# Differential values of an encoder trunk: one token tile after the other, high and low weight halves side by side

## The chip, the cores and the metric

The kernel runs on one core of a Trainium2 chip. The metric is the device time in microseconds (us). Before the change it is 1755.69 us, the median of 3 runs (1755.67 to 1756.33).

The core has a matrix engine (TensorE, PE), which multiplies a stationary 128x128 operand with a moving operand of up to 512 columns and adds the result up in PSUM; a vector engine (VectorE, DVE); a scalar engine (ScalarE, ACT); GpSimd (POOL); and SyncE (SP), which here issues most of the DMAs. PEld in the profile is the loading of the stationary operand, which lies beside PE's products.

## The reference

The program is a trunk of two layers over 512 tokens and a model width of 1024. In each layer differential attention, a convolution module and a neighbourhood attention run on the same normalised input, are merged by gates, and an FFN follows. The change touches one part, the values of the differential attention (4 heads of 128 columns):

```python
h = rmsnorm(x, norm)                       # 512 x 1024
va = (h @ w_in)[:, 1024:1536]              # values, 512 x 512: 4 heads x 128
v = va.reshape(B, S, HA, DV_A).transpose(0, 2, 1, 3)
...
a = softmax(q1 k1) - lam * softmax(q2 k2)  # for each head
o = einsum('bhqk,bhkd->bhqd', a, v)
```

The kernel computes a float32 product from fp32r operands: each operand is split into a high and a low half (`split`), and three products are added up, high by high, high by low and low by high.

## The kernel before

**Tiles.** The normalised input `self.h` is held as 8 chunks of 128 model columns (KD = 8), each as a high and a low half of 128 x 512 tokens, all in SBUF. `values` (L605 and below) computes the values of two heads, 256 columns, for all 512 tokens; `diff_v` calls it for group 0 (heads 0 and 1) and group 1 (heads 2 and 3). With two layers that is 4 calls. In each call the tokens are four tiles of 128; a tile's high or low half of one chunk is the stationary operand, and 256 columns of weights stream past it.

**The weights of a call** are 8 chunks of 128x256. `weights` loads four of them with one DMA (512 KB) into a raw buffer `wr`, and `split` makes the high half `wh` with a copy on ACT (L143) and the low half `wl` with a subtraction on DVE (L157). There are three buffers of each of `wr`, `wh` and `wl`, used in turn by all parts of the layer; a buffer is free once its last reader is done. A call takes two of each.

**The loops of a call.** The accumulators are two PSUM buffers `mm` of 128 x 2 x 256, each for two token tiles; there are three `mm` buffers in all. With the first four chunks the loop runs over the two accumulators, the chunks and the tiles of the accumulator; with the last four over chunks and then all four tiles. For each chunk and tile there are three products of 256 columns: L621 high tokens by `wh`, L623 high tokens by `wl`, L625 low tokens by `wh`. After the last one, four copies on ACT and four subtractions on DVE move the sums from PSUM into `v`, as a high and a low half of 256 columns each.

**What sets the order.** PE's order is the one that the program is written in (its schedule is manual). The order of ACT, DVE, POOL and SP comes from a scheduler by priorities; the load and split of weights have a priority that is up to 400 places ahead of where they are written (`high_priority`). The attention is cut into pieces that run from a queue: `chunk` counts, and every fourth `chunk` calls `tick`, which lets a waiting piece of attention issue its instructions between the products. `values` calls `chunk` 16 times, so there are 4 ticks in a call.

**What stands around a call.** In each layer the order is the projections of differential head 0 (`diff_in`: Q, then K), the values of group 0, head 1, a gate (`gate_c`), head 2, the values of group 1, head 3. In the first call the pieces are those of the neighbourhood attention (`natten_unit`): scores (L800), which DVE adds to a bias and reduces (L719), exponentials and scalings on ACT (`natten_b`, `natten_e`), transposes on PE, their copies `natten_pt` as a high half on ACT and a low half on DVE, and the product with its values on PE (L745, `natten_av`, `natten_mm`). In the second call they are those of the differential attention (`diff_sc`, `diff_av`). DVE also runs the taps of the convolution (`conv_z`, L160) and the rotation of Q and K (`diff_rp`, `diff_t`).

Of the kernel before, what the change touches and what calls it, by code (L numbers as in the profile page):

```python
# [11 lines left out]
F32 = mybir.dt.float32  # L12
F32R = mybir.dt.float32r
I32 = mybir.dt.int32
AF = mybir.ActivationFunctionType
ALU = mybir.AluOpType
# [4 lines left out]
P = 128  # L21
# [5 lines left out]
KD = 8  # L27
# [34 lines left out]
class Net:  # L62
# [539 lines left out]

        yield from self.norm(st[0], CB, (3, 1), done)

    def values(self, ap, parts):  # L605


        mm = self.nc.tensor.matmul
        accs = [self.ps("mm", (P, 2, 256)) for _ in range(2)]
        for o in range(0, KD, 4):  # L610
            wh, wl = self.weights(ap[:, o * 256:(o + 4) * 256], 1024)
            both = [(k, t) for k in range(o, o + 4) for t in range(4)]
            if o == 0:

                both.sort(key=lambda kt: kt[1] // 2)
            for n, (k, t) in enumerate(both):
                s = slice((k - o) * 256, (k - o + 1) * 256)
                out = accs[t // 2][:, t % 2, :]
                ts = slice(t * P, (t + 1) * P)

                mm(out, self.h[k][:, 0, ts], wh[:, s], start=k == 0 and t % 2 == 0,  # L621
                   stop=False, skip_group_check=True)
                mm(out, self.h[k][:, 0, ts], wl[:, s], start=False, stop=False,  # L623
                   skip_group_check=True)
                mm(out, self.h[k][:, 1, ts], wh[:, s], start=False,  # L625
                   stop=k == KD - 1 and t % 2 == 1, skip_group_check=True)
                if n % 2:
                    self.chunk()
        vs = []
        for acc in accs:  # L630
            v = self.sb("v", [P, 2, 512], F32R)
            for t in range(2):
                for hi, lo, a in parts(v[:, t], acc[:, t]):
                    self.split(hi, lo, a)
            vs.append(v)
        return vs

    def natten_in(self, pr, st, ys):
# [190 lines left out]

    def diff_v(self, g, st):  # L830
        self.phase = "diff"
        st["v", g] = self.values(self.a["w_va"][self.i, g], lambda v, a: ((v[:, 0:256], v[:, 256:512], a),))

    def diff_unit(self, head, qt, st4, k2, st, box, ys):

# [686 lines left out]
```

## Time and profile before

| | |
|---|---|
| median of 3 runs | 1755.69 us |
| profiled execution | 1756.09 us |
| its span in the profile | 1754.3 us |
| DMA, mean over the span | 145 GB/s |
| products on PE | 8970 |

The profiled execution is 1.8 us longer than its span, which counts from the first to the last instruction. The granted clock of PE is in the highest tenth in all 40 slices of the span. In rows of the timeline the first number is the start, the second the duration, both in us; "f32 x8" at the end means that eight instructions of one form stand in one row, and the brackets give the idle time before the row and what ended it. A product is drawn from its start to its modelled end, so that products overlap; the distance from one start to the next is the time that it takes in the stream.

In the rows of the windows each window has its length, then for PE, PEld, DVE, ACT and POOL the busy time in us with the number of instructions, then the granted clock, the share of DMA and its GB/s.

### The profile page before, as it was taken

Reading aid. Unit: us, or ns where it says so; the run is one execution under the profiler, and the core shown is the slowest. Engines: PE = TensorE matmul, PEld = TensorE weight load, DVE = VectorE, ACT = ScalarE, POOL = GpSimd, SP = SyncE. Lnnn points to the kernel's source line nnn. Section 1 sums busy time; section 2 is a strip of 40 time slices with the busy share of each in tenths; the row PEclk is TensorE's granted clock in tenths of the full one; section 3 lists DMA queues with packets and bytes.
Section 4 is the critical chain, followed back from the end, with each engine's and each line's share of the span. In section 5 each row is a group of like instructions: output and inputs, shape, how many; then the busy total and the mean of one; then the engine's idle time right before and its main releaser. Section 6 shows DMA issues by size and latency. Waiting matters only on the chain.

```text
span 1754.3 us, 25072 instructions
## 1 busy us (share of the span) xinstructions
PE 1747.3 (100%) x8970; PEld 1490.2 (85%) x8970; DVE 1421.7 (81%) x2346; ACT 964.4 (55%) x1729; POOL 104.0 (6%) x114
## 2 busy tenths in 40 slices
PE   9999999999999999999999999999999999999998
PEld 7888888888888888888888898888888988888887
DVE  7967987998799687797776688889887985977876
ACT  5566545226577275574545665553365763745654
POOL 0000000000121020100000000000001210101000
PEclk9999999999999999999999999999999999999999
DMA  6575641334767365543446655323256764755332
GB/s 230 159 192 158 162 126 46 112 100 140 230 162 186 118 171 155 142 119 131 156 130 164 194 150 153 111 73 96 93 176 199 183 172 121 179 143 157 96 105 97
DMA packets 114781, 253.82 MB, mean 145 GB/s; under 512 B 16864, under 2 KB 23776, under 8 KB 114656
## 3 DMA queue, kind: packets, MB, share of 16 engines
q1 hardware_dynamic: 101264, 227.83, 42.3%
q0 software_dynamic: 12672, 23.07, 8.1%
q8 instruction: 71, 1.16, 0.3%
q10 hardware_dynamic: 720, 1.31, 0.2%
q14 instruction: 54, 0.44, 0.1%
HBM read 215.46 MB, written 7.34 MB: 127 GB/s over the span
## 4 chain that ended last, share of the span: by engine, by line
PE 97%; DVE 1%; DMA 1%; ACT 1%; SPq 0%; issue 0%; POOL 0%; POOLq 0%; ACTq 0%; DVEq 0%
PE ffn_mm L1013 6%; PE ffn_sc L1013 6%; PE ffn_mm L180 4%; PE ffn_mm L179 4%; PE ffn_mm L181 4%; PE ffn_mm L1016 3%; PE ffn_sc L1016 3%; PE mergea_mm L180 2%; PE mergea_mm L181 2%; PE mergea_mm L179 2%; PE ffn_tr L1013 2%; PE natten_mm L179 2%; PE natten_mm L180 2%; PE gateb_mm L180 2%; PE gateb_mm L181 2%; PE gateb_mm L179 2%
## 5 line engine op out<-in xcount | busy, mean ns | idle before, releaser
L160 DVE SCALAR_TENSOR_TENSOR conv_z<-glu_z,pre_par,conv_z 128x512 f32<-128x512 f32 x240 | 179.6, 748 | 3.4
L143 ACT ACTIVATE ffn_wh<-ffn_wr 128x1024 fp32r<-128x1024 f32 (+1 forms) x92 | 92.7, 1021 | 99.5 <-PE ffn_mm L180 63.4
L157 DVE TENSOR_TENSOR ffn_wl<-ffn_wr,ffn_wh 128x1024 fp32r<-128x1024 f32 (+1 forms) x92 | 107.1, 1175 | 20.8 <-ACT ffn_wh L143 20.4
L979 POOL DMA_DIRECT2D ffn_qk<-w_fu x88 | 78.0, 992 | 589.3 <-DMA ffn_qk<-w_fu 323.7
L143 ACT ACTIVATE mergea_wh<-mergea_wr 128x1024 fp32r<-128x1024 f32 (+1 forms) x32 | 27.1, 846 | 96.8 <-PE mergea_mm L180 79.6
L157 DVE TENSOR_TENSOR ffn_t<-ffn_mm,wo_rb 128x512 f32<-128x512 f32 (+1 forms) x46 | 31.1, 677 | 51.6 <-PE ffn_mm L181 51.6
L157 DVE TENSOR_TENSOR ffn_wl<-ffn_qk,ffn_wh 128x1024 fp32r<-128x1024 f32 x44 | 53.7, 1220 | 11.0 <-ACT ffn_wh L143 10.9
L143 ACT ACTIVATE diff_a<-diff_sc,diff_s 128x512 f32<-128x512 f32 x32 | 22.0, 688 | 71.6 <-DVE diff_s L893 71.6
L143 ACT ACTIVATE ffn_wh<-ffn_qk 128x1024 fp32r<-128x1024 f32 x44 | 46.7, 1061 | 26.8 <-PE ffn_mm L180 16.2
L179 PE MATMUL ffn_mm<-ffn_v,ffn_wh 128*128 128x512 f32 x132 | 51.4, 389 | 0.0
L180 PE MATMUL ffn_mm<-ffn_v,ffn_wh 128*128 128x512 f32 x132 | 51.4, 389 | 0.0
L181 PE MATMUL ffn_mm<-ffn_v,ffn_wl 128*128 128x512 f32 x132 | 51.3, 389 | 0.0
L179 PE MATMUL ffn_mm<-ffn_y,ffn_wh 128*128 128x512 f32 x132 | 51.3, 389 | 0.0
L180 PE MATMUL ffn_mm<-ffn_y,ffn_wh 128*128 128x512 f32 x132 | 51.3, 389 | 0.0
L181 PE MATMUL ffn_mm<-ffn_y,ffn_wl 128*128 128x512 f32 x132 | 51.3, 389 | 0.0
L143 ACT ACTIVATE natten_wh<-natten_wr 128x1024 fp32r<-128x1024 f32 x24 | 25.4, 1058 | 42.2 <-issue 15.5
L1013 PE MATMUL ffn_sc<-wo_h,ffn_wh 128*128 128x512 f32 x176 | 48.0, 394 | 0.0
L157 DVE TENSOR_TENSOR ffn_t<-ffn_t,ffn_e 128x256 f32<-128x256 f32 x84 | 46.3, 551 | 1.0 <-ACT ffn_e L143 0.9
L893 DVE TENSOR_REDUCE diff_s<-diff_sc 128x1 f32<-128x512 f32 x64 | 42.1, 683 | 2.2 <-PE diff_sc L800 2.2
L1013 PE MATMUL ffn_mm<-wo_h,ffn_wh 128*128 128x512 f32 x160 | 43.6, 394 | 0.0
L225 POOL TENSOR_TENSOR diff_rc<-diff_sm,pre_power 128x4 f32<-128x4 f32 x8 | 8.9, 1115 | 561.8 <-DVE diff_sm L160 503.2
L143 ACT ACTIVATE natten_b<-natten_b,natten_s 128x256 f32<-128x256 f32 x64 | 30.4, 499 | 20.4 <-DVE natten_s L719 20.3
(894 smaller groups left out, 6050.1 us busy)
## 6 DMA issues: line engine op xcount, KB each, us to landing
ffn_qk<-w_fu POOLq DMA_DIRECT2D x88, 256.0 KB, 6.6
ffn_wr<-w_fg SPq DMA_DIRECT2D x44, 512.0 KB, 4.4
ffn_wr<-w_fd SPq DMA_DIRECT2D x32, 448.0 KB, 3.8
ffn_r<-w_fu SPq DMA_DIRECT2D x44, 256.0 KB, 3.1
ffn_qk<-w_fg SPq DMA_DIRECT2D x44, 256.0 KB, 3.3
ffn_qk<-w_fu SPq DMA_DIRECT2D x44, 256.0 KB, 3.4
natten_wr<-w_in SPq DMA_DIRECT2D x16, 512.0 KB, 4.2
diff_wr<-w_in SPq DMA_DIRECT2D x16, 512.0 KB, 4.3
```

The source lines that it names most:

```text
L143: i = self.nc.scalar.activation(out, in_, func, **kw)
L157: return self.nc.vector.tensor_tensor(out, a, b, op)
L160: return self.nc.vector.scalar_tensor_tensor(out, a, s, b, op0, op1)
L179: mm(out, wh, ah, start=first, stop=False, **kw)
L180: mm(out, wh, al, start=False, stop=False, **kw)
L181: mm(out, wl, ah, start=False, stop=last, **kw)
L225: nc.gpsimd.tensor_tensor(col, ms, self.power, ALU.pow)
L893: nc.vector.tensor_reduce(out=m[:, u:u + 1], in_=sc, op=ALU.max, axis=AX.X, negate=True)
L979: nc.gpsimd.dma_start(q, wu[:, lo], accum_op=ALU.add)
L1013: mm(out, wh[:, c], bs[k][b], start=first and k == 0, stop=False, skip_group_check=True)
L1016: mm(out[:, 0], wl[:, c], bs[k][b][:, 0], start=False, stop=k == 3, skip_group_check=True)
```

## The change

`values` is written anew. The token tile is now the outermost loop. The high and the low half of a weight chunk lie side by side in one buffer of 128 x 2 x 2 x 256 (two chunks a buffer; the buffers tagged `wh` and `wl` hold the first and the second pair of chunks of a load). For each tile the high tokens of the 8 chunks are multiplied with 512 columns (L624), the high and the low weights at once, into a PSUM buffer of 2 x 256; then the low tokens of the 8 chunks with the 256 columns of the high weights (L628), into the first half of it. The two halves are added when the tile is moved out: a copy on ACT (high half of the first 256), a subtraction on DVE, and a further addition on DVE of the second 256 columns. Each tile has its own `mm` buffer, so the third tile takes the buffer of the first. Loads and splits of all weights are written ahead of the loop; a load is split in two pieces of 128 x 2 x 256. There are still 16 calls of `chunk`.

```diff
@@ -602,37 +602,39 @@
 
         yield from self.norm(st[0], CB, (3, 1), done)
 
-    def values(self, ap, parts):
+    def values(self, ap):
 
 
         mm = self.nc.tensor.matmul
-        accs = [self.ps("mm", (P, 2, 256)) for _ in range(2)]
-        for o in range(0, KD, 4):
-            wh, wl = self.weights(ap[:, o * 256:(o + 4) * 256], 1024)
-            both = [(k, t) for k in range(o, o + 4) for t in range(4)]
-            if o == 0:
-
-                both.sort(key=lambda kt: kt[1] // 2)
-            for n, (k, t) in enumerate(both):
-                s = slice((k - o) * 256, (k - o + 1) * 256)
-                out = accs[t // 2][:, t % 2, :]
-                ts = slice(t * P, (t + 1) * P)
-
-                mm(out, self.h[k][:, 0, ts], wh[:, s], start=k == 0 and t % 2 == 0,
-                   stop=False, skip_group_check=True)
-                mm(out, self.h[k][:, 0, ts], wl[:, s], start=False, stop=False,
+        ws = []
+        with self.tc.high_priority(offset=min(self.w_ahead, self.tc.cur_priority - self.p0)):
+            for o in range(0, KD, 4):
+                raw = self.sb("wr", [P, 2, 2, 256])
+                self.nc.sync.dma_start(raw.rearrange("p a b c -> p (a b c)"),
+                                       ap[:, o * 256:(o + 4) * 256])
+                for n, tag in enumerate(("wh", "wl")):
+                    w = self.sb(tag, [P, 2, 2, 256], F32R)
+                    self.split(w[:, :, 0], w[:, :, 1], raw[:, n])
+                    ws += [w[:, k] for k in range(2)]
+        vs = []
+        for t in range(4):
+            out = self.ps("mm", (P, 2, 256))
+            hs = [(a[:, 0, t * P:(t + 1) * P], a[:, 1, t * P:(t + 1) * P]) for a in self.h]
+            for k, (hi, lo) in enumerate(hs):
+                mm(out, hi, ws[k], start=k == 0, stop=False, skip_group_check=True)
+                if k % 4 == 3:
+                    self.chunk()
+            for k, (hi, lo) in enumerate(hs):
+                mm(out[:, 0], lo, ws[k][:, 0], start=False, stop=k == KD - 1,
                    skip_group_check=True)
-                mm(out, self.h[k][:, 1, ts], wh[:, s], start=False,
-                   stop=k == KD - 1 and t % 2 == 1, skip_group_check=True)
-                if n % 2:
+                if k % 4 == 3:
                     self.chunk()
-        vs = []
-        for acc in accs:
-            v = self.sb("v", [P, 2, 512], F32R)
-            for t in range(2):
-                for hi, lo, a in parts(v[:, t], acc[:, t]):
-                    self.split(hi, lo, a)
-            vs.append(v)
+            if t % 2 == 0:
+                v = self.sb("v", [P, 2, 512], F32R)
+                vs.append(v)
+            hi, lo = v[:, t % 2, 0:256], v[:, t % 2, 256:512]
+            self.split(hi, lo, out[:, 0])
+            self.tt(lo, lo.bitcast(F32), out[:, 1], ALU.add)
         return vs
 
     def natten_in(self, pr, st, ys):
@@ -829,7 +831,7 @@
 
     def diff_v(self, g, st):
         self.phase = "diff"
-        st["v", g] = self.values(self.a["w_va"][self.i, g], lambda v, a: ((v[:, 0:256], v[:, 256:512], a),))
+        st["v", g] = self.values(self.a["w_va"][self.i, g])
 
     def diff_unit(self, head, qt, st4, k2, st, box, ys):
 
```

Three places show how the order of instructions changes. All are in the first call of layer 1.

On PE, the last scores of the attention piece in the middle of the call, and what follows. `diff_mm` are PSUM buffers, `glu_h` the tokens, `natten_sc` the scores' buffer. Before:

```order
L800 MATMUL natten_sc_1590<-natten_qk_1161 128x256
L800 MATMUL natten_sc_1590<-natten_x_1162,natten_qk_1161 128x256
L621 MATMUL diff_mm_1505<-diff_wh_1603,glu_h_490 128x256
L623 MATMUL diff_mm_1505<-diff_wl_1604,glu_h_490 128x256
L625 MATMUL diff_mm_1505<-diff_wh_1603,glu_h_490 128x256
L621 MATMUL diff_mm_1505<-diff_wh_1603,glu_h_490 128x256
```

After:

```order
L802 MATMUL natten_sc_1588<-natten_qk_1161 128x256
L802 MATMUL natten_sc_1588<-natten_x_1162,natten_qk_1161 128x256
L624 MATMUL diff_mm_1603<-diff_wh_1507,glu_h_386 128x512
L624 MATMUL diff_mm_1603<-diff_wh_1507,glu_h_411 128x512
L624 MATMUL diff_mm_1603<-diff_wl_1510,glu_h_427 128x512
L624 MATMUL diff_mm_1603<-diff_wl_1510,glu_h_474 128x512
```

Before, the products behind the scores went on into the accumulator of the first half of the call, `diff_mm_1505`. Now the third tile begins there, in the new buffer `diff_mm_1603`, which is the memory of the first tile's `diff_mm_1521` and waits for its eviction.

On DVE, the rows from the end of a split of K (`diff_rp`, `diff_kh`) to the first row of the attention's output `natten_y`. Before:

```order
L157 TENSOR_TENSOR diff_rp_1403<-diff_t_1410,diff_kh_1415 128x512
L160 SCALAR_TENSOR_TENSOR conv_z_370<-glu_z_321,pre_par_67,conv_z_370 128x512
L157 TENSOR_TENSOR diff_rp_1482<-diff_rp_1482,diff_r_1323 128x512
L157 TENSOR_TENSOR diff_t_1488<-diff_t_1488,diff_rp_1482 128x512
L157 TENSOR_TENSOR diff_wl_1766<-diff_wr_1764,diff_wh_1765 128x1024
L157 TENSOR_TENSOR diff_rp_1481<-diff_t_1488,diff_kh_1493 128x512
L157 TENSOR_TENSOR natten_y_1079<-natten_mm_1561,natten_y_1079 64x512
```

After:

```order
L157 TENSOR_TENSOR diff_rp_1403<-diff_t_1410,diff_kh_1415 128x512
L160 SCALAR_TENSOR_TENSOR conv_z_370<-glu_z_321,pre_par_67,conv_z_370 128x512
L157 TENSOR_TENSOR diff_v_1538<-diff_mm_1521,diff_v_1538 128x256
L157 TENSOR_TENSOR diff_rp_1482<-diff_rp_1482,diff_r_1323 128x512
L157 TENSOR_TENSOR diff_v_1538<-diff_v_1538,diff_mm_1521 128x256
L157 TENSOR_TENSOR diff_t_1488<-diff_t_1488,diff_rp_1482 128x512
L157 TENSOR_TENSOR diff_v_1538<-diff_mm_1542,diff_v_1538 128x256
L157 TENSOR_TENSOR diff_v_1538<-diff_v_1538,diff_mm_1542 128x256
L157 TENSOR_TENSOR diff_rp_1481<-diff_t_1488,diff_kh_1493 128x512
L157 TENSOR_TENSOR natten_y_1079<-natten_mm_1559,natten_y_1079 64x512
```

The split `diff_wl` of 128x1024, which is the low half of the next head's K weights, is gone from there. In its place stand four rows that move the first and the second tile out (`diff_mm_1521` and `diff_mm_1542`, into `diff_v_1538`), the first of them two rows ahead of the rotation `diff_rp_1482`, and its addition behind it. The split stands later, with these rows around it:

```order
L157 TENSOR_TENSOR diff_v_1620<-diff_mm_1603,diff_v_1620 128x256
L157 TENSOR_TENSOR diff_v_1620<-diff_v_1620,diff_mm_1603 128x256
L157 TENSOR_TENSOR diff_wl_1744<-diff_wr_1742,diff_wh_1743 128x1024
L157 TENSOR_TENSOR gatec_wl_1843<-gatec_wr_1841,gatec_wh_1842 128x1024
L721 ISA natten_b_1641,natten_s_1645<-natten_sc_1646,natten_b_1641 128x256
```

It follows the third tile's eviction and is ahead of the attention's reductions (L721, which was L719 before).

On ACT, the rows from the first copy of the call's end to the split of the following Q weights. `diff_wh` is the high half of weights, `gatec_wh` that of a gate. Before:

```order
L143 ACTIVATE diff_v_1685<-diff_mm_1505 128x256
L143 ACTIVATE gatec_wh_1864<-gatec_wr_1863 128x1024
L143 ACTIVATE diff_v_1685<-diff_mm_1505 128x256
L143 ACTIVATE natten_b_1656,natten_s_1660<-natten_b_1656,natten_s_1660 128x256 x2
L143 ACTIVATE diff_v_1690<-diff_mm_1506 128x256
L143 ACTIVATE natten_b_1656<-natten_b_1656,natten_s_1660 128x256 x2
L143 ACTIVATE natten_e_1657,natten_s_1660<-natten_e_1657,natten_s_1660 128x256 x2
L143 ACTIVATE diff_v_1690<-diff_mm_1506 128x256
L143 ACTIVATE natten_pt_1721<-natten_tr_1716 128x512
L143 ACTIVATE natten_e_1657<-natten_e_1657,natten_s_1660 128x256 x2
L143 ACTIVATE natten_pt_1729<-natten_tr_1724 128x512
L143 ACTIVATE diff_wh_1929<-diff_wr_1928 128x1024
```

After:

```order
L143 ACTIVATE diff_v_1620<-diff_mm_1603 128x256
L143 ACTIVATE diff_wh_1743<-diff_wr_1742 128x1024
L143 ACTIVATE gatec_wh_1842<-gatec_wr_1841 128x1024
L143 ACTIVATE natten_e_1572<-natten_e_1572,natten_s_1575 128x256 x2
L143 ACTIVATE diff_v_1620<-diff_mm_1624 128x256
L143 ACTIVATE natten_b_1641,natten_s_1645<-natten_b_1641,natten_s_1645 128x256 x2
L143 ACTIVATE natten_e_1642,natten_s_1645<-natten_e_1642,natten_s_1645 128x256 x2
L143 ACTIVATE natten_b_1641<-natten_b_1641,natten_s_1645 128x256 x2
L143 ACTIVATE natten_e_1642<-natten_e_1642,natten_s_1645 128x256 x2
L143 ACTIVATE natten_pt_1699<-natten_tr_1694 128x512
L143 ACTIVATE diff_wh_1907<-diff_wr_1906 128x1024
L143 ACTIVATE natten_pt_1707<-natten_tr_1702 128x512
```

The K split `diff_wh_1743` is now behind the third tile's copy and ahead of the gate's; the split of the Q weights (`diff_wh_1907`) now stands ahead of the second `natten_pt`, where it stood behind it.

Outside the two calls of each layer, and the stretch after each, the order is the same.

## The prediction

> **What bounds the kernel now.** The table of busy time comes first, then the list of what TensorE (PE) waited for.
>
> ```profile
> PE 1747.3 (100%) x8970; PEld 1490.2 (85%) x8970; DVE 1421.7 (81%) x2346; ACT 964.4 (55%) x1729; POOL 104.0 (6%) x114
> PE pre_av L331 <- DVE pre_zeror L404: 1.1, 1, 1.1
> PE diff_sc L800 <- ACT diff_e L143: 0.2, 1, 0.2
> ```
>
> PE is busy for 1747.3 of 1754.3 us, and its two visible waits come to 1.3 us. A product is drawn longer than its place in the stream, so "busy" can hide a short stall; the starts are the better clock. So two things decide here: how far apart the starts of the products of `values` stand, and whether the change makes PE wait for the first time.
>
> The timeline of PE in the first call (layer 1, group 0), and of an FFN stretch that already mixes 512 and 256 columns, gives the distances:
>
> ```profile
> 141.90 0.28 PE L623 MATMUL diff_mm<-diff_wl,glu_h 128*128 128x256 f32 x1
> ...
> 147.42 0.28 PE L625 MATMUL diff_mm<-diff_wh,glu_h 128*128 128x256 f32 x1
> 147.54 1.07 PE L745 MATMUL natten_mm<-natten_pt,natten_v 128*128 128x192 f32 x8
> 148.44 0.30 PE L800 MATMUL natten_sc<-natten_qk 128*128 128x256 f32 x1
> ...
> 654.48 1.09 PE L1013 MATMUL ffn_sc<-wo_h,ffn_y 128*128 128x512 f32 x4
> 655.40 0.63 PE L1016 MATMUL ffn_sc<-wo_h,ffn_y 128*128 128x256 f32 x4
> 655.88 0.63 PE L1013 MATMUL ffn_mm<-wo_rp,ffn_pt 128*128 128x512 f32 x2
> ```
>
> From 141.90 to 147.42 lie 46 steps (48 products, less the slow first one): 5.52 / 46 = 0.120 us for each 256-column product. In the FFN four 512-column products take 655.40 - 654.48 = 0.92, 0.230 each, and four narrow ones 0.48, 0.120 each. Two narrow products cost 0.240, one wide one 0.230.
>
> **The change part by part.** *PE.* A call issued 8 x 4 x 3 = 96 narrow products: 96 x 0.120 = 11.52 us. Now it issues 32 wide and 32 narrow ones: 32 x 0.230 + 32 x 0.120 = 11.20 us. That is 0.32 us less, **1.28 us in four calls**; the columns streamed stay the same. Nothing else leaves PE, and the attention pieces between the tiles are the same in number and order.
>
> *The weight splits* are four of 128x512 on each engine instead of two of 128x1024. They are bounded by the 1024 row (1.22 us on DVE) and the 512 rows (0.69): 4 x 0.69 - 2 x 1.22 = 0.3 us more of DVE a call. Both chunks are split before the call begins in the old order as in the new, so I take nothing on the path.
>
> *Holding the weights.* Before, the first chunk's buffers came free half way through the call, and the split for the next head's K projection ran there. Now all four tiles read both chunks, so that split runs at the end of the call, and ACT and DVE run it ahead of the attention pieces (the order rows above). The rows of before at that place, DVE first, then ACT:
>
> ```profile
> 147.23 0.74 DVE L160 SCALAR_TENSOR_TENSOR conv_z<-glu_z,pre_par,conv_z 128x512 f32<-128x512 f32 x1
> 148.71 0.69 DVE L157 TENSOR_TENSOR diff_rp<-diff_rp,diff_r 128x512 f32<-128x512 f32 x1 [0.73 <-DMA diff_rp<-diff_rp]
> 149.44 0.69 DVE L157 TENSOR_TENSOR diff_t<-diff_t,diff_rp 128x512 f32<-128x512 f32 x1
> 150.05 1.22 DVE L157 TENSOR_TENSOR diff_wl<-diff_wr,diff_wh 128x1024 fp32r<-128x1024 f32 x1
> 151.18 0.69 DVE L157 TENSOR_TENSOR diff_rp<-diff_t,diff_kh 128x512 fp32r<-128x512 f32 x1
> ...
> 156.67 0.17 DVE L725 RECIPROCAL natten_s<-natten_s 128x2 f32<-128x2 f32 x1 [1.62 <-ACT natten_e L143]
> 158.22 0.42 DVE L157 TENSOR_TENSOR diff_v<-diff_mm,diff_v 128x256 fp32r<-128x256 f32 x1 [1.38 <-ACT diff_v L143]
> 158.56 0.41 DVE L719 CUSTOM_DVE_ANT_0 natten_b<-natten_sc,natten_b 128x256 f32<-128x256 f32 x1
> ...
> 164.57 0.69 DVE L157 TENSOR_TENSOR natten_pt<-natten_tr,natten_pt 128x512 fp32r<-128x512 f32 x1 [0.59 <-ACT natten_pt L143]
> ```
>
> ```profile
> 156.45 0.19 ACT L143 ACTIVATION_READ_ACCUMULATOR natten_e<-natten_e,natten_s 128x1 f32 x1
> 156.87 0.91 ACT L143 ACTIVATE natten_e<-natten_e,natten_s 128x256 f32<-128x256 f32 x2 [0.23 <-DVE natten_s L725]
> 157.80 0.38 ACT L143 ACTIVATE diff_v<-diff_mm 128x256 fp32r<-128x256 f32 x1
> 158.08 1.05 ACT L143 ACTIVATE gatec_wh<-gatec_wr 128x1024 fp32r<-128x1024 f32 x1
> 159.03 0.37 ACT L143 ACTIVATE diff_v<-diff_mm 128x256 fp32r<-128x256 f32 x1
> 159.30 0.51 ACT L143 ACTIVATE natten_b<-natten_b,natten_s 128x256 f32<-128x256 f32 x1
> ...
> 163.95 0.58 ACT L143 ACTIVATE natten_pt<-natten_tr 128x512 fp32r<-128x512 f32 x1
> 164.43 1.06 ACT L143 ACTIVATE diff_wh<-diff_wr 128x1024 fp32r<-128x1024 f32 x1
> ```
>
> ```profile
> 165.22 1.08 PE L745 MATMUL natten_av<-natten_pt,natten_v 128*128 128x192 f32 x8
> ```
>
> *First new wait, tile 2.* The third tile writes the first tile's PSUM buffer and waits for DVE's add into it. PE gets there at 141.7 + 2 x (8 x 0.23 + 8 x 0.12) + 0.9 (natten) + 1.0 (eight scores) = 149.2. On DVE the subtraction fits before the DMA wait, but the add stands behind `diff_rp`, which starts at 148.71 with its DMA: 148.71 + 0.6 + 0.42 = 149.7. PE waits 0.5 us.
>
> *Second new wait, the second `natten_pt`.* Follow the two engines. DVE does four evictions of tiles 0 and 1 in place of the 1.13 us split at 150.05, about as long; the natten chain stays where it was, within 0.2 us earlier, so ACT is free at 156.4. ACT then does tile 2's copy (0.28 from start to start), the K split (0.95), the gate split (0.95), two `natten_e` (0.85): 159.4. DVE takes the K low half when ACT has finished the high one, from 157.8, and the gate's, 1.14 each: 160.05. Only then come the four natten reductions (0.34 each, until 161.5), whose first stood at 158.56 before. ACT's four exponentials follow from 160.5 (0.49 each): 162.6. Four scalings (0.40): 164.2. First `natten_pt` copy, 0.48: 164.7. Then the next head's Q split, which is now ahead of the second copy: 0.95, 165.7. Second copy 0.58, 166.2. DVE has the Q split's low half from 165.8 (1.14), then the second `natten_pt` low half from 166.9, done at **167.6**. Before, it was done at 164.57 + 0.69 = 165.3.
>
> PE needs it at the sixth of the eight products at 165.22: 165.8, which before was half a microsecond after it was ready. Without waits the new kernel would be there at 165.8 - 0.3 = 165.5. It is there at 167.6: the first call ends **1.8 us late in layer 1**, the 0.5 us included. Behind PE's waiting product are natten transposes and the rest of the K projection; nothing else is released by them early enough to matter.
>
> In layer 2 the DMA lands earlier against the same products:
>
> ```profile
> 1017.41 0.69 DVE L157 TENSOR_TENSOR diff_rp<-diff_rp,diff_r 128x512 f32<-128x512 f32 x1
> ...
> 1033.26 0.69 DVE L157 TENSOR_TENSOR natten_pt<-natten_tr,natten_pt 128x512 fp32r<-128x512 f32 x1 [0.59 <-ACT natten_pt L143]
> 1034.63 1.08 PE L745 MATMUL natten_av<-natten_pt,natten_v 128*128 128x192 f32 x8
> ```
>
> The products stand 869.4 us later than in layer 1 and the DVE rows 868.7. The DMA no longer holds the add, so the chain gains about 0.3 us: **1.5 us late**. In layer 1 a wait of before is paid off:
>
> ```profile
> 174.56 0.40 PE L800 MATMUL diff_sc<-diff_x,diff_qk 128*128 128x512 f32 x1
> 175.19 0.50 PE L800 MATMUL diff_sc<-diff_qk 128*128 128x512 f32 x1 [0.23 <-ACT diff_e L143]
> ```
>
> This step took 0.63 instead of 0.23: a PE that comes 1.8 us later finds `diff_e` done, and 0.4 us return.
>
> *Second call of each layer.* No transposes of natten stand there; the same adds and splits go on a fuller DVE:
>
> ```profile
> 141.70:158.00 16.30, 16.30 (x132) 15.96 (x130) 12.58 (x26) 8.25 (x20) 0.00 (x0) 1.00 0.71 190
> 175.00:192.00 17.00, 16.81 (x77) 13.81 (x78) 16.60 (x29) 9.21 (x20) 0.00 (x0) 1.00 0.59 150
> 192.00:208.00 16.00, 16.00 (x127) 15.59 (x126) 14.74 (x27) 8.27 (x18) 0.00 (x0) 1.00 0.68 187
> 195.59 1.22 DVE L157 TENSOR_TENSOR diff_wl<-diff_wr,diff_wh 128x1024 fp32r<-128x1024 f32 x1 [1.19 <-ACT diff_wh L143]
> 207.88 0.28 PE L179 MATMUL diff_av<-diff_pt,diff_v 128*128 128x256 f32 x1
> ```
>
> The third column is DVE. Each call adds four adds of 0.42 and 0.3 of splits, 2.0 us: DVE has 3.7 us idle in the first stretch, 1.3 in the third. But the K split (1.2 us) moves behind the call there too. The next wait for the adds is that of the head-3 Q projection for tile 1's, 12 products of 0.12 after 207.88 - 0.3, at 209.0. Counting DVE's rows on from 195.59, the add is done at 208.6; margin 0.4. I take 0.1 us of waits against the saving of 0.3.
>
> **Sum**, against the profiled execution's 1756.1 us: layer 1, 1.8 - 0.4 - 0.2; layer 2, 1.5 - 0.2; together **+2.5 us**. The median of the runs shown is 1755.7, 0.4 below that execution: 1758.2, 0.14% up.
>
> **The rivals.** *A, no new wait holds PE.* If ACT and DVE finish the second `natten_pt` by 165.5, only the saving is left: 1755.7 - 1.3 = 1754.4. For it: PE waits nearly nowhere now. Against: the chain above is 2.1 us over, and no idle row of ACT or DVE lies in it to be used. 22%.
>
> *B, DVE sets the pace in the second calls: slower.* Its place is tile 1's add, its price up to the 2.0 us of new DVE work less 0.4 of margin, 1.6 a call, from the point where the add is over 0.4 us later than counted. For it: 16.60 of 17 us busy just before. Against: DVE's 1.19 us of idle at 195.59, which is tied to PE. 2.5 + 2 x 1.6 = 5.7 over: 1761.4. 24%.
>
> *C, the time goes by the number of products: faster.* If every product took 0.12 whatever its width, a call would save 32 x 0.12 = 3.84, 15.4 in all: 1740.3. Against: 0.92 for four wide ones. 3%. The Trainium skill, "TensorE: Matmul & The Clock Gate", section "Back-to-back issue gap", gives about 81 ns and 131 ns a product for 128 and 512 columns in a stream with loads. By it, with 98 ns put between them for 256, the saving would be 96 x 98 - 32 x (131 + 98) = 2.1 us a call, an estimate, 1747.3 in all. The trace disagrees with its 131: 230.
>
> That the wide product costs two narrow ones, so that the change saves nothing, lies within the forecast's range: +1.3 us.
>
> **How the numbers follow.** Forecast 51%, A 22%, B 24%, C 3%. A measurement of this kernel can tell about 0.2%, 3.5 us, from no change. A lies within it, and of the forecast all but 6 of its 51: same 0.67, slower 0.24 + 0.06 = 0.30, faster 0.03. The range, 1754.0 to 1762.0, takes in A and B with 0.4 and 0.6 around them.
>
> **What would show it.** The profile of the changed kernel should have 32 products fewer in each call, 8842 in all instead of 8970; wide starts 0.23 apart in `values`; a wait of PE `natten_av` for DVE `natten_pt` of 1 to 2 us in each layer, and a smaller one of `diff_mm` for DVE `diff_v`. If neither is there, A holds; if the wait is at the head-3 Q projection, B; starts below 0.2 apart would make the whole sum wrong.

## The result and the profile after

The changed kernel takes 1758.78 us, the median of 21 runs (1757.87 to 1759.59), against 1756.21 us for 21 runs of the kernel before (1755.39 to 1756.74): 2.57 us more, ratio 1.0016 with a 95% interval from 1.0010 to 1.0022. The forecast was +2.5 us.

The list of what TensorE waited for, which held two entries before:

```profile
PE natten_av L747 <- DVE natten_pt L157: 2.0, 2, 1.0
PE pre_av L331 <- DVE pre_zeror L404: 1.1, 1, 1.1
PE pre_mm L179 <- ACT pre_y L143: 0.6, 1, 0.6
PE diff_mm L624 <- DVE diff_v L157: 0.2, 1, 0.2
```

The numbers are the total, the count and the longest wait. `natten_av` waits once in each layer, and the third tile (`diff_mm` L624) once visibly, in layer 2. `pre_av` and `pre_mm` lie in the opening, which the change doesn't touch.

PE's timeline of the first call, with the products of `values` and the place of the wait:

```profile
143.34 0.62 PE L624 MATMUL diff_mm<-diff_wl,glu_h 128*128 128x512 f32 x2
143.80 0.62 PE L624 MATMUL diff_mm<-diff_wh,glu_h 128*128 128x512 f32 x2
...
144.94 0.40 PE L628 MATMUL diff_mm<-diff_wl,glu_h 128*128 128x256 f32 x2
145.18 0.40 PE L628 MATMUL diff_mm<-diff_wh,glu_h 128*128 128x256 f32 x2
...
150.22 0.28 PE L802 MATMUL natten_sc<-natten_x,natten_qk 128*128 128x256 f32 x1
150.49 0.70 PE L624 MATMUL diff_mm<-diff_wh,glu_h 128*128 128x512 f32 x2
...
166.19 1.08 PE L747 MATMUL natten_av<-natten_pt,natten_v 128*128 128x192 f32 x5
168.26 0.58 PE L747 MATMUL natten_av<-natten_pt,natten_v 128*128 128x256 f32 x3 [1.00 <-DVE natten_pt L157]
168.69 0.49 PE L737 MATMUL natten_tr<-pre_ident,natten_b 128*128 128x128 f32 x3
```

Two wide products take 143.80 - 143.34 = 0.46, two narrow ones 0.24: 0.23 and 0.12 each, as forecast. The third tile starts 0.27 after the last score instead of 0.12, so it waits 0.15, though the list and the row show nothing. From the first `natten_av` product to the transposes behind the eighth it is now 168.69 - 166.19 = 2.50 us. The same group of eight ahead of the call took 0.91 in this profile (141.09 to 142.00). So the stall is 1.6 us, though the row shows 1.00: the fifth product is drawn to its modelled end, and that hides 0.6 of it.

In layer 2 the third tile waits longer:

```profile
1020.33 0.28 PE L802 MATMUL natten_sc<-natten_x,natten_qk 128*128 128x256 f32 x1
1020.79 0.70 PE L624 MATMUL diff_mm<-diff_wh,ple_h 128*128 128x512 f32 x2 [0.18 <-DVE diff_v L157]
```

It starts 0.46 after the last score, 0.34 late, of which the row shows 0.18.

What DVE and ACT did ahead of the late `natten_av` product of layer 1:

```profile
158.50 1.23 DVE L157 TENSOR_TENSOR diff_wl<-diff_wr,diff_wh 128x1024 fp32r<-128x1024 f32 x1
159.64 1.22 DVE L157 TENSOR_TENSOR gatec_wl<-gatec_wr,gatec_wh 128x1024 fp32r<-128x1024 f32 x1
160.78 0.42 DVE L721 CUSTOM_DVE_ANT_0 natten_b<-natten_sc,natten_b 128x256 f32<-128x256 f32 x1
...
165.43 0.69 DVE L157 TENSOR_TENSOR natten_pt<-natten_tr,natten_pt 128x512 fp32r<-128x512 f32 x1 [1.92 <-ACT natten_pt L143]
166.38 1.23 DVE L157 TENSOR_TENSOR diff_wl<-diff_wr,diff_wh 128x1024 fp32r<-128x1024 f32 x1 [0.26 <-ACT diff_wh L143]
167.52 0.68 DVE L157 TENSOR_TENSOR natten_pt<-natten_tr,natten_pt 128x512 fp32r<-128x512 f32 x1
```

```profile
157.13 0.38 ACT L143 ACTIVATE diff_v<-diff_mm 128x256 fp32r<-128x256 f32 x1
...
164.82 0.57 ACT L143 ACTIVATE natten_pt<-natten_tr 128x512 fp32r<-128x512 f32 x1
165.30 1.05 ACT L143 ACTIVATE diff_wh<-diff_wr 128x1024 fp32r<-128x1024 f32 x1
166.25 0.58 ACT L143 ACTIVATE natten_pt<-natten_tr 128x512 fp32r<-128x512 f32 x1
```

The K split (158.50) and the gate split stand ahead of the attention's reductions, and the Q split (166.38) ahead of the second `natten_pt` low half, which is done at 168.20. PE's sixth product starts at 168.26.

**Where the time went.** Outside `values`, PE starts the same sequence of instructions in all these kernels, so its place in the stream can be compared row by row. The table gives how much later PE stands (minus: earlier) than in a second profile of the kernel before (`before_again`, below), at the same instruction, in us. L1 and L2 are the layers, call 1 and call 2 the calls of `values` in them; `after_again` is a second profile of the changed kernel. It is worked out from the starts in PE's timelines:

```
PE instruction (time in before_again)   before   after   after_again
natten_tr ahead of call 1, L1   141.49   -0.59   +0.51   -0.63
natten_tr behind natten_av      166.72   -0.58   +1.97   +0.83
diff_sc                         182.00   +0.04   +1.96   +0.84
diff_av, end of call 2, L1      207.82   +0.06   +1.69   +0.52
natten_tr ahead of call 1, L2  1010.26   +0.06   +1.85   +0.52
natten_sc, end of call 1, L2   1024.53   +0.06   +1.91   +0.56
gatec_mm behind natten_av      1040.02   +0.06   +3.52   +2.17
diff_mm behind call 2, L2      1080.10   +0.05   +3.19   +1.85
```

The opening differs between executions of one kernel by up to 1.1 us. From the first call on, the changed kernel loses 1.46 us in the first call of layer 1 in both profiles, wins 0.3 in the second, loses 1.65 in the first call of layer 2 and wins 0.33 in the second: 3.19 - 0.51 = 2.68 and 1.85 + 0.63 = 2.48, around the 2.57 of the medians. The loss of a first call is nearly the sum of three parts: 0.32 saved by the products, the wait of the third tile (0.15 in layer 1, 0.34 in layer 2) and the stall at `natten_av` (1.6). That gives 1.43 and 1.62.

### The profile page after: what moved, and what is told of

It reads as the page before. It is cut to its first block, busy times and chain, and to the rows that moved or that the text cites. A ratio compares the mean times of both kernels' runs of the same rounds, so it can differ in the third digit from the quotient of the medians.

```text
span 1757.5 us, 24856 instructions
## 1 busy us (share of the span) xinstructions
PE 1747.6 (99%) x8842; PEld 1483.9 (84%) x8842; DVE 1426.9 (81%) x2370; ACT 965.7 (55%) x1737; POOL 104.2 (6%) x114
## 4 chain that ended last, share of the span: by engine, by line
PE 94%; DVE 2%; ACT 1%; DMA 1%; SPq 0%; issue 0%; POOL 0%; POOLq 0%; ACTq 0%; DVEq 0%
PE ffn_mm L1015 6%; PE ffn_sc L1015 6%; PE ffn_mm L180 4%; PE ffn_mm L181 4%; PE ffn_mm L179 4%; PE ffn_mm L1018 3%; PE ffn_sc L1018 3%; PE mergea_mm L181 2%; PE mergea_mm L180 2%; PE mergea_mm L179 2%; PE ffn_tr L1015 2%; PE diff_sc L802 2%; PE gatec_mm L180 2%; PE gatec_mm L179 2%; PE gatec_mm L181 2%; PE gateb_mm L180 2%
```

## The experiments

The forecast's theory: the time is lost where the second `natten_pt` low half comes late, behind weight splits that were moved ahead of it. The rivals: the added DVE additions are the price wherever they stand, or it is the holding of the weights. Each time below is a median, set against that of the kernel before in the same rounds.

**x1: the Q split back behind `natten_pt`.** The changed kernel with one dependence added (the line that sets `self.hold` to None at the start is left out here):

```diff
 def split(...):
+        i = self.last = self.act(hi, src, AF.Copy)
 def weights(...):
-            self.low = self.split(hi[:, :n], lo[:, :n], raw[:, :n], then)
+            self.low = self.split(hi[:, :n], lo[:, :n], raw[:, :n], then or self.hold)
+            self.hold = None
 def natten_unit(...):
             ps.append(pp)
+            self.last_pt = self.last
 def diff_in(...):
+            if head == 2 and s == 0:
+                self.hold = self.keep
             ps = self.proj(off + head * P)
+            if head == 1 and s == 0:
+                self.keep = self.last_pt
```

> The changed kernel with one thing moved: in each layer the ACT split of head 2's Q weights is ordered behind the second natten_pt copy of the first call (it stood ahead of it). Theory (the late natten_pt is the loss, and the Q split ahead of it is the last 1.1 us of it): the second natten_pt low half is done about 166.7 on the clock of the changed kernel's profile instead of 168.2, the sixth natten_av product is due at 166.76, so both 1.0 us waits go (under 0.2 left each); layer 1 gets less back at diff_e, 0.3. Time 1.7 us below the changed kernel, 0.9 us over the kernel before (ratio 1.0005). Rival 1 (the four adds a call are the price, wherever they stand): still 2.6 over, ratio 1.0015, with the wait at another place. Rival 2 (the K and gate splits ahead of the reductions are enough to make natten_pt late): natten_av keeps over 0.5 us of wait in each layer, time 1.5 to 2 over.

Measured: 1755.96 against 1756.08, ratio 0.9999 (0.9990 to 1.0008). That is 2.6 to 2.8 us below the changed kernel's two medians (1758.56 and 1758.78), more than the 1.7 expected. ACT and DVE, then PE, in its profile:

```profile
164.66 1.06 ACT L143 ACTIVATE natten_pt<-natten_tr 128x512 fp32r<-128x512 f32 x2
165.62 1.05 ACT L143 ACTIVATE diff_wh<-diff_wr 128x1024 fp32r<-128x1024 f32 x1
```

```profile
159.48 1.22 DVE L157 TENSOR_TENSOR gatec_wl<-gatec_wr,gatec_wh 128x1024 fp32r<-128x1024 f32 x1
160.62 0.42 DVE L722 CUSTOM_DVE_ANT_0 natten_b<-natten_sc,natten_b 128x256 f32<-128x256 f32 x1
...
165.27 1.29 DVE L157 TENSOR_TENSOR natten_pt<-natten_tr,natten_pt 128x512 fp32r<-128x512 f32 x2 [1.92 <-ACT natten_pt L143]
166.70 1.23 DVE L157 TENSOR_TENSOR diff_wl<-diff_wr,diff_wh 128x1024 fp32r<-128x1024 f32 x1
```

```profile
166.02 1.18 PE L749 MATMUL natten_av<-natten_pt,natten_v 128*128 128x192 f32 x8
167.03 0.49 PE L738 MATMUL natten_tr<-pre_ident,natten_b 128*128 128x128 f32 x3
```

The eight products are in one row again, 1.01 us to the transposes, 0.10 more than without a wait. The K and gate splits still stand ahead of the reductions (the gate's at 159.48, the first reduction at 160.62) and the adds are all there, yet the stall of 1.6 us at `natten_av` is gone. So rival 1 falls. Rival 2 falls too, but narrowly: `natten_pt` is done at 166.56, and the product needs it at about 166.6. The K and gate splits used up the room, and the Q split overran it. The size was expected wrong because I took the 1.0 us that the row shows; by the starts 1.5 us go in each layer (2.50 against 1.01). From the first call to the end of the last one PE wins 0.60 us on `before_again`, of the 1.28 that the products save: the third tile still waits 0.15 and 0.34, and 0.1 is left at `natten_av` in each layer.

**x7: the same order put into the kernel before.** The same lines, but the dependence turned round: `self.behind(self.hold, self.last)` puts the second `natten_pt` copy behind the Q split.

> The kernel before, with only the converse order: in each layer the second natten_pt copy of the first call is put behind the ACT split of head 2's Q weights. No wide products, no adds, no held weights. Theory: the second natten_pt low half is done about 166.8 instead of 165.3, PE needs it at 165.8: a wait of 1.0 us at natten_av in each layer, 0.4 of it given back at diff_e in layer 1; 1.6 us over the kernel before, ratio 1.0009. Rival (adds or held weights are needed for the loss): no wait at natten_av, ratio 1.0000.

Measured: 1757.80 against 1756.08, 1.7 us more, ratio 1.0008 (0.9999 to 1.0017). DVE and PE:

```profile
165.65 1.23 DVE L157 TENSOR_TENSOR diff_wl<-diff_wr,diff_wh 128x1024 fp32r<-128x1024 f32 x1 [1.05 <-ACT diff_wh L143]
166.79 0.68 DVE L157 TENSOR_TENSOR natten_pt<-natten_tr,natten_pt 128x512 fp32r<-128x512 f32 x1
```

```profile
166.17 0.75 PE L749 MATMUL natten_av<-natten_pt,natten_v 128*128 128x192 f32 x5
167.53 0.59 PE L749 MATMUL natten_av<-natten_pt,natten_v 128*128 128x256 f32 x3 [0.61 <-DVE natten_pt L157]
```

A wait of the same kind is there without one wide product, one add or a held weight, though a shorter one: from the call's start PE falls behind by 0.88 us in layer 1 and 0.63 in layer 2, where the changed kernel stalls 1.6. The interval touches 1, so the time alone wouldn't show it; the rows do. What was expected back at `diff_e` did not come. On the contrary, between the first call of layer 1 and the end of the second PE loses another 0.47, most of it at the scores of the following heads (`diff_sc`), behind this row of DVE:

```profile
174.62 0.69 DVE L157 TENSOR_TENSOR diff_rp<-diff_rp,diff_r 128x512 f32<-128x512 f32 x1 [2.52 <-DMA diff_rp<-diff_rp]
```

In `before_again` that row starts at 172.10 (below), 2.52 earlier, though PE is only 1.24 behind here. The last three of its DMAs were issued at 167.82 here and at 167.16 there, so most of the difference lies behind their issue.

**x2: narrow products, weights held.** The kernel before, with both weight loads ahead and two tiles at a time over all 8 chunks:

```diff
-        for o in range(0, KD, 4):
-            wh, wl = self.weights(ap[:, o * 256:(o + 4) * 256], 1024)
...
+        ws = [self.weights(ap[:, o * 256:(o + 4) * 256], 1024) for o in range(0, KD, 4)]
+        for n, (a, k, t) in enumerate((a, k, t) for a in range(2) for k in range(KD) for t in range(2)):
+            wh, wl = ws[k // 4]
...
```

> The kernel before with its 256-column products and no adds, but with both weight loads of a call taken ahead and held: two token tiles at a time over all 8 chunks. Here the scheduler leaves the Q split behind the second natten_pt, and sets the K split among the first attention unit's exponentials. Theory (the order at natten_pt decides, not that the weights are held): natten_av waits under 0.4 us a layer, time within 0.7 us of the kernel before, ratio 0.9997 to 1.0004. Rival (holding the weights, so that the K split comes late, is itself the price): natten_av or the K projection waits 0.8 us or more in each layer, 1.5 us or more over, ratio 1.0009 or more.

Measured: 1756.82 against 1756.08, ratio 1.0003 (0.9994 to 1.0012). From the first call to the end of the last one PE stands within 0.01 us of `before_again` at every row of the table above. Its median stands 0.5 us over that of `before_again`; in the two profiles the difference arises behind the calls. It is not explained, and the interval holds no change. The K split is late here too, and costs nothing in the stream:

```profile
156.69 1.23 DVE L157 TENSOR_TENSOR diff_wl<-diff_wr,diff_wh 128x1024 fp32r<-128x1024 f32 x1 [1.61 <-ACT diff_wh L143]
...
163.85 0.69 DVE L157 TENSOR_TENSOR natten_pt<-natten_tr,natten_pt 128x512 fp32r<-128x512 f32 x1
165.13 0.69 DVE L157 TENSOR_TENSOR natten_pt<-natten_tr,natten_pt 128x512 fp32r<-128x512 f32 x1 [0.59 <-ACT natten_pt L143]
```

Holding the weights moves the K split; it does not by itself set the loss. The Q split stays behind the second `natten_pt` copy here (ACT starts them at 164.99 and 164.51), so holding the weights alone does not move it ahead either; what does so in the changed kernel is not shown. It was not tried whether a fourth pair of weight buffers would bring the K split back to its old place in the changed kernel.

**x3: without the adds.** The line `self.tt(lo, lo.bitcast(F32), out[:, 1], ALU.add)` is taken out, so the high tokens by low weights are missing from the values.

> The changed kernel without the DVE addition of the second 256 columns (it leaves the high tokens by low weights out of the values). Theory: the add is a small part of the chain; the wait of the third tile (0.2 us a layer) goes, natten_av still waits 0.8 to 1.0 us a layer; 0.7 us below the changed kernel, 1.9 over the kernel before, ratio 1.0011. Rival (the 16 adds, 5.4 us of DVE, are the price): natten_av waits under 0.3 us and the time is 1 us or more below the kernel before, ratio 0.9994 or less.

Measured: 1758.59 against 1756.08, ratio 1.0013 (1.0004 to 1.0022): 2.5 over, by the time no different from the changed kernel. From the first call to the end PE loses 2.25 us, against 2.48 and 2.68 in the two profiles of the changed kernel. `natten_av` waits as before in this kernel's list:

```profile
PE natten_av L746 <- DVE natten_pt L157: 2.0, 2, 1.0
```

So the 16 adds are worth 0.2 to 0.4 us; the rival falls, and my 0.7 was too much. The third tile starts 0.12 behind the scores in both layers, so its waits of 0.15 and 0.34 are gone, but little of that is kept: the first call of layer 1 still ends 1.37 late (1.46 with the adds) and that of layer 2 1.56 (1.65). In layer 2 0.3 us are lost at the eight transposes ahead of `natten_av` instead, which take 1.07 us from first to last start against 0.77.

**The kernel before and the changed kernel once more.** Both unchanged, for the noise of the comparison and for second profiles.

> The kernel before, unchanged, for the noise of the comparison and for a second profile of its opening. Theory 1 (the start of the span differs from execution to execution with the landing of the first loads): ratio 1.0000, and the first values call starts anywhere from 141.7 to 142.7 us. Theory 2 (the opening belongs to each kernel): the call starts at 141.7 again, within 0.15.

> The changed kernel, unchanged, for a second profile of it. Theory 1 (the opening differs from execution to execution): the first values call starts anywhere from 141.7 to 142.8 us; theory 2 (it belongs to each kernel): 142.8 within 0.15. Either way from that start to the end of the second layer's second call it gains 2.1 us on the kernel before, with 1.0 us of wait at natten_av in each layer, and the ratio is 1.0015.

Measured: `before_again` 1756.29 against 1756.47 (ratio 1.0000, 0.9990 to 1.0009), `after_again` 1758.56 (1.0011, 1.0002 to 1.0020). The opening goes with the execution: the transposes ahead of the first call start at 140.90 in the first profile of before and 141.49 in the second, 142.00 and 140.86 for the changed kernel. In the changed kernel's two profiles the second input tile lands at different times; ACT's row in each:

```profile
6.79 0.73 ACT L143 ACTIVATE glu_v<-pre_x,pre_a 128x512 fp32r<-128x512 f32 x1 [1.43 <-DMA pre_x<-xT]
```

```profile
5.45 0.73 ACT L143 ACTIVATE glu_v<-pre_x,pre_a 128x512 fp32r<-128x512 f32 x1
```

In the two profiles of the kernel before it is not this tile: ACT starts on it at 5.40 and 5.50. There PE's first four products behind `pre_av` stand further apart: they take from 4.59 to 5.62 in the first profile and from 4.63 to 6.29 in the second, at a granted clock of 1.00 in both. Why is not shown.

Another landing bears on the forecast. DVE's row behind the wait of `diff_sc`, in the first and the second profile of the kernel before:

```profile
173.03 0.69 DVE L157 TENSOR_TENSOR diff_rp<-diff_rp,diff_r 128x512 f32<-128x512 f32 x1 [1.79 <-DMA diff_rp<-diff_rp]
```

```profile
172.10 0.69 DVE L157 TENSOR_TENSOR diff_rp<-diff_rp,diff_r 128x512 f32<-128x512 f32 x1 [0.91 <-DMA diff_rp<-diff_rp]
```

ACT had written `diff_rp` at the same time in both (it starts on it at 165.38 and 165.34), and SyncE issued the first of the rotation's four DMAs at 166.00 and 165.95. But the issue of a weight load (`diff_wr`) that it took up next lasted 1.35 us in the first and 0.39 in the second, so the other three DMAs were issued at 168.17 and 167.16. Why that issue lasted longer is not shown. In the first, the result came 0.93 us later while PE was 0.59 earlier; the reduction behind it held `diff_e`, and PE stood until its lead was gone (-0.58 to +0.04 in the table). In the second PE has no such wait.

**x5: evictions early as well.** x1, with each tile's eviction under a priority 100 places ahead:

```diff
-            self.split(hi, lo, out[:, 0])
-            self.tt(lo, lo.bitcast(F32), out[:, 1], ALU.add)
+            with self.tc.high_priority(offset=100):
+                self.split(hi, lo, out[:, 0])
+                self.tt(lo, lo.bitcast(F32), out[:, 1], ALU.add)
```

> The run with head 2's Q split behind natten_pt, and in addition the eviction of each token tile of the values given a priority 100 places ahead, so that DVE adds the first tile before it multiplies the rotation. Theory: the third tile's start no longer waits for DVE (0.2 to 0.4 us a layer go), natten_av does not wait either; all of the PE saving of 1.3 us is left in the stream, and the time is 0.5 us below that run: 1755.4, ratio 0.9996. Rival (the shorter stream is given back elsewhere, where DVE is fullest): same time as that run, with a new wait in the second call or behind it.

Measured: 1755.65 against 1756.47, ratio 0.9997 (0.9988 to 1.0006). That is as expected in size, but the interval holds no change, and the stream tells another story. From the first call to the end PE wins only 0.37 us on `before_again`, of the 1.28 that the shorter products save; x1 won 0.60. In layer 2 the third tile no longer waits (PE goes from -0.43 to -0.77), and then 0.46 is lost at the transposes, which wait for ACT:

```profile
1027.47 0.49 PE L739 MATMUL natten_tr<-pre_ident,natten_b 128*128 128x128 f32 x3
1028.03 0.84 PE L739 MATMUL natten_tr<-pre_ident,natten_e 128*128 128x128 f32 x4
```

```profile
1025.31 1.04 ACT L143 ACTIVATE diff_wh<-diff_wr 128x1024 fp32r<-128x1024 f32 x1
1026.26 1.04 ACT L143 ACTIVATE gatec_wh<-gatec_wr 128x1024 fp32r<-128x1024 f32 x1
...
1027.47 0.90 ACT L143 ACTIVATE natten_e<-natten_e,natten_s 128x256 f32<-128x256 f32 x2
```

The K and gate splits stand ahead of the two scalings that the transposes need. The wait moved, so the rival was nearer, though its place (in the second call or behind it) was not the one.

**x6: the gate split behind `natten_pt` too.** x5 and, in `gate_c`:

```diff
+        if m == 0:
+            self.hold = self.keep
         ps = self.proj(OFF_G + 2 * D + m * P)
```

> The last run (Q split behind natten_pt, evictions early), and in addition the ACT split of the first gate's weights ordered behind the second natten_pt copy of the first call. Theory (what is left of the PE saving is lost at natten_tr, which waits for ACT's scalings of natten_e behind the K and gate splits: 0.2 us in layer 1, 0.5 in layer 2): these waits go, and from the start of the first call to the end of the last one PE gains 0.9 to 1.3 us on the kernel before, against the second profile of it, where the last run gained 0.3; ratio 0.9993. Rival (the gate's weights come too late, or another wait takes the place): PE waits at gatec_mm, and the gain stays at 0.3 us or less.

Measured: 1759.47 against 1756.10, 3.4 us more, ratio 1.0021 (1.0012 to 1.0030). The theory held for the first call: PE wins the full 0.34 us in each layer (+0.48 to +0.14 in layer 1, at the rows of the table) with no wait at `natten_tr` or `natten_av`. Then it loses 2.1 us in layer 1 and 2.3 in layer 2, further on, at the scores of head 2. So the rival's half sentence, that another wait takes the place, was the right one. Two lines of its list of waits:

```profile
PE diff_sc L807 <- ACT diff_e L143: 1.9, 2, 1.0
PE diff_sc L807 <- ACT diff_a L143: 1.2, 2, 0.6
```

The gate split now stands at 166.09 on DVE (158.82 in x5), ahead of the work on head 2. ACT's `diff_a` waits for DVE until 181.38, and the scheduler has put two splits of value weights between it and `diff_e`, where x5 has them behind `diff_e`:

```profile
181.38 0.69 ACT L143 ACTIVATE diff_a<-diff_sc,diff_s 128x512 f32<-128x512 f32 x1 [2.26 <-DVE diff_s L904]
...
182.06 0.62 ACT L143 ACTIVATE diff_wh<-diff_wr 128x512 fp32r<-128x512 f32 x1
182.58 0.62 ACT L143 ACTIVATE diff_wl<-diff_wr 128x512 fp32r<-128x512 f32 x1
183.10 0.68 ACT L143 ACTIVATE diff_e<-diff_sc,diff_s 128x512 f32<-128x512 f32 x1
```

## Why the prediction was right, step by step

**The products.** Right: 0.23 and 0.12, 8842 products; the stream alone is 0.27 to 0.35 us shorter a call, as the second calls of both layers and x6 show, against 0.32 forecast.

**Tile 2.** The mechanism was right, the size in layer 1 too large: 0.5 us forecast, 0.15 measured (0.27 less 0.12). The step that failed is that `diff_rp` would hold DVE until its DMA at 148.71. In `after_again`, whose opening was that of the profile the forecast used (-0.63 and -0.59), it runs at 148.19 without a wait:

```profile
148.19 0.68 DVE L157 TENSOR_TENSOR diff_rp<-diff_rp,diff_r 128x512 f32<-128x512 f32 x1
148.79 0.41 DVE L157 TENSOR_TENSOR diff_v<-diff_v,diff_mm 128x256 fp32r<-128x256 f32 x1
```

**The second `natten_pt`.** Right in its links: the order of the splits, the reductions after them, the Q split ahead of the second low half. With the later opening (142.00 - 140.90 = 1.10) taken off, it was done at 168.20 - 1.10 = 167.1; forecast 167.6. The first call ends 1.46 us late instead of 1.8: ACT came free for the third tile's copy at 157.13 - 1.10 = 156.0, where 156.4 was counted, and the rest of the chain kept its length. What tile 2 waited for was nearly contained in this longer wait, as forecast: without it (x3) the call ends 0.09 earlier. x1 and x7 show that the order of the Q split is the last link: take it out and the stall goes, put it alone into the old kernel and a shorter one comes (0.88 and 0.63). The rest of the 1.6 belongs to the K and gate splits that stand ahead of it, by the rows; no run takes out these alone.

**Layer 2.** The step "the DMA no longer holds the add, so the chain gains 0.3" was wrong, since the DMA held it in neither layer of the changed kernel's profiles. Against PE, DVE does not stand earlier in layer 2 but 0.2 later (in `after_again` its rows lie 870.1 us behind those of layer 1, PE's 869.9), and the third tile waits 0.34. The first call there ends 1.65 late, not 1.5.

**The wait paid off at `diff_e`.** Wrong as a gain of the change: the wait comes and goes with the execution. It costs the first profile of before 0.6 us and x7 0.4, and it is in neither `before_again` nor x2, whose order there is the same. Against `before_again` the changed kernel gets nothing back (+0.83 to +0.84). This term was 0.4 of the sum. How often executions have that wait, the record does not say.

**The second calls.** Right: no wait at the head-3 Q projection; 0.32 us won in each, where 0.2 was forecast. So rival B, DVE setting the pace there, did not come. x6 shows a limit of that kind ahead of the second call: with one split of 1.2 us moved from 158.8 to 166.1, and the order that the scheduler made of it, 2.1 and 2.3 us go. Rival A is what x1 and x5 are, and rival C falls with the 0.23.

That the sum came out to a tenth is luck, because the errors cancel: 1.46 + 1.65 - 2 x 0.32 = 2.5 measured, 1.8 + 1.5 - 0.4 - 0.4 = 2.5 forecast. The forecast counted 0.2% as the least change that can be told from none; with 21 runs of each kernel the interval is 0.06% to either side, so the 0.16% is told from none.

No kernel tried beats the kernel before beyond its interval: the best, x5, is at 0.9997 (0.9988 to 1.0006), and all that the wide products can give here is 1.3 us, 0.07%.

## What to carry to other kernels

Here PE hardly ever waited, and a change that shortens its stream by 0.3 us in a call of about 15 was decided by what the scheduler did with the off-path work. So when a change holds a buffer longer, compare the order of the instructions before and after, find the split that now comes late, and follow the in-order queues of the two engines behind it to the next instruction that PE needs. Measure a stall from start to start, not by the wait that the row shows. And before a term rests on a wait behind a DMA, look at a second execution.

## What the runs showed that was not expected

The landing of one rotation (`diff_rp`) differs by 0.93 us between two executions of the same kernel: three of its four DMAs were issued 1.01 later, behind a weight load whose issue lasted 1.35 us instead of 0.39. Between two executions of the changed kernel the opening differs by 1.14 us, with a second input tile on which ACT starts 1.34 later; PE carries such a shift to the end unless a wait on other engines absorbs it. A visible wait of 1.00 us stood for a stall of 1.6.
